# Layer 0's mixer in seven-product units, with two DMA sums each, and the state space half of the output projection among the output gate's products

## The chip, the core and the metric

The kernel runs on one core of one Trainium2 chip. The time is what the device takes for one execution of the whole program, in microseconds (us). TensorE (PE in the profile) multiplies; VectorE (DVE), ScalarE (ACT) and GpSimd (POOL) do the elementwise work; SyncE (SP) issues most of the DMAs. Each engine takes its instructions in the order of its own queue, and semaphores make one engine wait for another.

## The reference

Two layers over 512 tokens of width 1024, all in float32. The change lies in layer 0's mixer: one input projection, split into a state space group (z, xbc, dt) and an mLSTM group (q, k, v, output gate, input and forget gate), whose outputs are concatenated for one output projection.

```python
def hybrid_mixer(h, w_in, conv_w, conv_b, dt_bias, a_log, d_skip, ssd_norm,
                 igate_bias, fgate_bias, mlstm_norm, w_out):
...
    z, xbc, dt_raw, qm, km, vm, om, ig, fg = split_cols(h @ w_in, HY_SPLITS)
    xbc = jax.nn.silu(causal_dwconv(xbc, conv_w, conv_b))
...
    y = y + xs * d_skip.astype(jnp.float32)[:, None]
    gate = jax.nn.silu(z.astype(jnp.float32)).reshape(b, L, SSD_GROUPS, -1)
    y = rms_norm(y.reshape(b, L, SSD_GROUPS, -1) * gate, ssd_norm.reshape(SSD_GROUPS, -1))
    y = y.reshape(b, L, SSD_WIDTH)
    hm = mlstm_chunked(qm.reshape(b, L, ML_HEADS, ML_QK_DIM), km.reshape(b, L, ML_HEADS, ML_QK_DIM),
                       vm.reshape(b, L, ML_HEADS, ML_V_DIM), ig + igate_bias, fg + fgate_bias, ML_CHUNK)
    hm = rms_norm(hm, mlstm_norm.reshape(ML_HEADS, ML_V_DIM)).reshape(b, L, ML_WIDTH)
    hm = hm * jax.nn.sigmoid(om.astype(jnp.float32))
    return jnp.concatenate([y, hm], axis=-1).astype(h.dtype) @ w_out
```

Widths: z 1024, xbc 1536, dt 16, q and k 512 each, v and the output gate 1024 each, two gates of 4; the output projection takes 2048 to 1024. Layer 0 runs a feed-forward block before and after the mixer, and so does layer 1 around its attention.

## The kernel before

**Products in two parts.** Every large product is made of float32 operands split into a high part (a rounding that ScalarE writes) and a low part (what VectorE has left after a subtraction): `split`, L236. `mm3`, L277, is three matmuls: high by high, high by low, low by high. A weight block (128 partitions x 1024 elements, 512 KB) comes by SP's queue into one of four raw buffers (`raw`, L251), and `form`, L257, writes its two parts into one of five form buffers. Both rings are walked in the order in which the program is written, so a buffer's next load or form waits for the last reader of its old content. The third way of `form`, L264 to L266, leaves the subtraction to a DMA: ScalarE writes the negated rounding, a DMA issued by GpSimd adds the raw block to it, and ScalarE writes the rounding. In the mixer of layer 0 it isn't used.

**Seven products.** In the feed-forward blocks most units are done by `seven`, L621: x and a block of weights are each cut in two by two quarters, and seven products of sums of quarters (names A11 to S4, L478) take the place of eight. `xforms`, L572, makes the seven forms of x; differences of weight quarters are made in place by VectorE. The feed-forward blocks and layer 1 have an order written out by a planner (`Plan`, L80) with costs and due times. Layer 0's mixer has none: it is written as generators, and `weave`, L53, gives out steps of one between steps of the other; the framework then orders each engine's queue by a simulated time line, in which what is written earlier goes first where it is ready.

**The mixer**, `hybrid`, L947, in four stretches. First `gates` and `conv` (L1012, six column blocks of 256), on 512-wide products of x times its gain (`xg`); the row of norms (`rrow`) is applied behind the product. Then `ssd` (L1202, 16 steps of 4 blocks by 4 groups of heads) is woven with `projections`: q and k by `gemm_feat`, v and the output gate by `gemm_tok`, L1068, four banks at a time. `decays`, L1235, gets rows of cumulated gates by a broadcast DMA on SP's queue, subtracts on VectorE (L1244), masks on GpSimd, takes the exponential on ScalarE and multiplies on VectorE (L1250, L1253); `outputs`, L1256, has the step's matmuls and their sums (L1268). One step is prepared ahead. Then `mlstm`, L1303, is woven with `gate` (z, L1034). At its end the gated heads are transposed and split (`pht`, L1000). `project`, L898, then runs all 16 row blocks of the output projection, in the order state space first half, mLSTM, state space second half, adds the result to the residual `xT` and prepares x for the next block (`prep`).

PSUM: four banks for large products, four for small ones (`aux`), and pairs of banks (`ps_two`) for the feed-forward units.

## Time and profile before

| | us |
|---|---|
| median of three runs | 2020.58 (2020.55 to 2025.87) |
| profiled execution, its own time | 2019.29 |
| span of that profile, first to last instruction | 2017.6 |
| mean granted clock of TensorE | 0.992 |

The page of a profile gives each engine's busy time and its share of the span, the chain of work that ended last, and groups of instructions: line, engine, operation, what is written from what (partitions x elements), count, then busy time and mean duration in ns, then the engine's idle time just before them and what ended it. Durations of neighbours on one engine overlap, so a price is better read from the distance between two starts in the timeline (start in us from the span's beginning, duration in us, engine, line, operation). L280 to L282 are the three matmuls of every large product. Rows of windows give busy time and counts in a stretch. The mixer of layer 0 lies between about 353 and 757 us.

### The profile page before, as it was taken

Reading aid. Unit: us, or ns where it says so; the run is one execution under the profiler, and the core shown is the slowest. Engines: PE = TensorE matmul, PEld = TensorE weight load, DVE = VectorE, ACT = ScalarE, POOL = GpSimd, SP = SyncE. Lnnn points to the kernel's source line nnn. Section 1 sums busy time; section 2 is a strip of 40 time slices with the busy share of each in tenths; the row PEclk is TensorE's granted clock in tenths of the full one; section 3 lists DMA queues with packets and bytes.
Section 4 is the critical chain, followed back from the end, with each engine's and each line's share of the span. In section 5 each row is a group of like instructions: output and inputs, shape, how many; then the busy total and the mean of one; then the engine's idle time right before and its main releaser. Section 6 shows DMA issues by size and latency. Waiting matters only on the chain.

```text
span 2017.6 us, 34412 instructions
## 1 busy us (share of the span) xinstructions
PE 1984.4 (98%) x13892; PEld 1800.6 (89%) x13892; DVE 1581.4 (78%) x2340; ACT 1170.2 (58%) x1716; POOL 270.1 (13%) x335
## 2 busy tenths in 40 slices
PE   8999999999999999999999999999999999999998
PEld 6999999787788888999998899999965678999998
DVE  6898878886547648988888898978679847988886
ACT  6666657442345434666565575756667644757565
POOL 1000101321101011010002010101215321101010
PEclk9999999999999999999999999999899999999999
DMA  7556566433331232666565356656754202656564
GB/s 210 136 148 167 150 164 148 125 107 115 103 96 63 82 97 63 168 157 162 155 152 149 94 148 167 161 153 160 191 116 105 53 16 69 157 158 165 150 168 115
DMA packets 214439, 265.49 MB, mean 132 GB/s; under 512 B 14140, under 2 KB 187400, under 8 KB 214280
## 3 DMA queue, kind: packets, MB, share of 16 engines
q1 hardware_dynamic: 193632, 190.87, 30.5%
q0 software_dynamic: 20448, 72.36, 19.2%
q8 instruction: 109, 1.79, 0.4%
q14 instruction: 50, 0.41, 0.1%
q10 hardware_dynamic: 200, 0.06, 0.0%
HBM read 188.77 MB, written 2.14 MB: 95 GB/s over the span
## 4 chain that ended last, share of the span: by engine, by line
PE 86%; DVE 5%; DMA 4%; issue 2%; ACT 1%; POOL 1%; SPq 0%; ACTq 0%; POOLq 0%; DVEq 0%
PE pA L281 9%; PE pA L280 9%; PE pA L282 9%; PE pD L280 5%; PE pD L281 5%; PE pD L282 5%; PE pB L280 2%; PE pB L281 2%; PE pB L282 2%; DMA form<-raw 2%; PE po L280 2%; PE po L282 2%; PE po L281 2%; PE ptok L280 2%; PE pu L282 2%
## 5 line engine op out<-in xcount | busy, mean ns | idle before, releaser
L502 DVE TENSOR_TENSOR form<-raw,form 128x1024 fp32r<-128x1024 f32 (+1 forms) x327 | 388.0, 1191 | 113.2 <-ACT form L500 112.3
L500 ACT ACTIVATE form<-raw 128x1024 fp32r<-128x1024 f32 (+1 forms) x327 | 334.6, 1027 | 177.3 <-DVE raw L495 120.6
L280 PE MATMUL pA<-xf,form 128*128 128x256 f32 x1152 | 322.1, 280 | 0.0
L281 PE MATMUL pA<-xf,form 128*128 128x256 f32 x1152 | 321.8, 279 | 0.0
L282 PE MATMUL pA<-xf,form 128*128 128x256 f32 x1152 | 321.4, 279 | 0.0
L495 DVE TENSOR_TENSOR raw<-raw 128x1024 f32<-128x1024 f32 (+2 forms) x241 | 283.6, 1180 | 17.4 <-DMA raw<-in_ffn_w_down 8.6
L530 POOL DMA_DIRECT2D form<-raw x136 | 116.9, 860 | 1202.7 <-ACT form L529 1142.4
L529 ACT ACTIVATE form<-raw 128x1024 fp32r<-128x1024 f32 (+1 forms) x136 | 140.1, 1031 | 140.3 <-PE pD L282 77.4
L280 PEld LDWEIGHTS pA<-xf,form 128*128 128x128 f32 x1152 | 216.4, 188 | 0.2
L282 PEld LDWEIGHTS pA<-xf,form 128*128 128x128 f32 x1152 | 216.1, 188 | 0.0
L281 PEld LDWEIGHTS pA<-xf,form 128*128 128x128 f32 x1152 | 215.8, 187 | 0.2
L281 PE MATMUL pA<-hid,form 128*128 128x256 f32 x704 | 198.6, 282 | 2.8 <-DVE hid L502 2.8
L280 PE MATMUL pA<-hid,form 128*128 128x256 f32 x704 | 198.8, 282 | 0.5 <-ACT hid L500 0.4
L282 PE MATMUL pA<-hid,form 128*128 128x256 f32 x704 | 197.4, 280 | 0.0
L280 PE MATMUL pD<-xf,form 128*128 128x256 f32 x576 | 161.2, 280 | 0.0
L281 PE MATMUL pD<-xf,form 128*128 128x256 f32 x576 | 161.2, 280 | 0.0
L282 PE MATMUL pD<-xf,form 128*128 128x256 f32 x576 | 161.0, 280 | 0.0
L495 DVE TENSOR_TENSOR ft<-ft 128x256 f32<-128x256 f32 (+2 forms) x288 | 146.1, 539 | 4.6 <-ACT ft L748 1.2
L531 ACT ACTIVATE form<-raw 128x1024 fp32r<-128x1024 f32 (+1 forms) x136 | 138.6, 1021 | 0.0
L281 PEld LDWEIGHTS pA<-hid,form 128*128 128x128 f32 x704 | 132.3, 188 | 4.7 <-DVE hid L502 4.6
L280 PEld LDWEIGHTS pA<-hid,form 128*128 128x128 f32 x704 | 132.6, 188 | 1.3 <-ACT hid L500 0.6
L282 PEld LDWEIGHTS pA<-hid,form 128*128 128x128 f32 x704 | 132.3, 188 | 0.0
(447 smaller groups left out, 5191.5 us busy)
## 6 DMA issues: line engine op xcount, KB each, us to landing
form<-raw POOLq DMA_DIRECT2D x120, 512.0 KB, 5.6
raw<-in_ffn_w_gate SPq DMA_DIRECT2D x88, 512.0 KB, 3.8
raw<-in_ffn_w_up SPq DMA_DIRECT2D x88, 512.0 KB, 4.0
raw<-in_ffn_w_down SPq DMA_DIRECT2D x64, 512.0 KB, 4.4
raw<-in_hy_w_in SPq DMA_DIRECT2D x44, 512.0 KB, 3.5
raw<-in_ffn_w_down SPq DMA_DIRECT2D x32, 384.0 KB, 3.4
raw<-in_hy_w_out SPq DMA_DIRECT2D x16, 512.0 KB, 3.3
form<-raw POOLq DMA_DIRECT2D x16, 384.0 KB, 4.2
```

Of the source, the lines that this page charges most:

```text
L280: mm(out, l[0], r[0], start=start, stop=False)
L281: mm(out, l[0], r[1], start=False, stop=False)
L282: mm(out, l[1], r[0], start=False, stop=stop)
L495: (self.p if pool else self.v)(n, lambda: e.tensor_tensor(out(), x(), y(), op=op), reads, writes)
L500: self.s(n, lambda: nc.scalar.activation(hi(), src(), AF.Copy), srck, hik)
L502: n, lambda: nc.vector.tensor_tensor(lo(), src(), hi().bitcast(F32), op=ALU.subtract), srck + hik, lok
L529: self.s(n, lambda: nc.scalar.activation(f()[:, 1], raw, AF.Copy, scale=-1.0), rawk, lok)
L530: self.plan.add("gpsimd", 0.85, lambda: nc.gpsimd.dma_start(f()[:, 1], raw, accum_op=ALU.add), rawk + lok, lok, 5.5)
L531: self.s(n, lambda: nc.scalar.activation(f()[:, 0], raw, AF.Copy), rawk, hik)
```

## The change

The products of v, k, z and the output gate become seven-product units of 512 columns (`seven_now`): two for v, one for k, two for z, two for the output gate. The seven forms of x, now with the norm applied, are made by `xforms_now` in four row groups, woven among convolution and q. In each unit the forms of two blocks go by the DMA sum; among convolution and q the second half of each weight block does (`early`). The scratch tiles of scan and mLSTM move into one large tile (`room`). The scan's and mLSTM's subtractions become biases of four narrower exponentials, and three of the scan's steps are prepared ahead instead of one. mLSTM's output is written over v, and its norm and the output gate are multiplied in behind the gate's products. `project` becomes a generator and is called twice: the state space half from two raw and two form buffers of its own (`side`), woven with the output gate's units, and the mLSTM half at the end. A second sum into the residual comes with the second call.

```diff
-NMIX = dict(mix0=10, mix1=15)
+NMIX = dict(mix0=12, mix1=15)
...
-        r = self.rings[which]
+        r = self.rings[self.side + which]
...
-        if self.stage == "mix1":
+        if self.stage == "mix0" and self.summing:
             nc.scalar.activation(f[:, 1], raw, AF.Copy, scale=-1.0)
             nc.gpsimd.dma_start(f[:, 1], raw, accum_op=ALU.add)
             nc.scalar.activation(f[:, 0], raw, AF.Copy)
...
-    def wload(self, src):
+    def wload(self, src, side=""):
 
         n = src.shape[0] // P
         for k in range(0, n, 4):
-            yield self.form(self.raw(src[k * P : (k + 4) * P].rearrange("(k p) n -> p k n", p=P), 4, 256))
+            self.summing, self.side = self.early and k == 4, side
+            f = self.form(self.raw(src[k * P : (k + 4) * P].rearrange("(k p) n -> p k n", p=P), 4, 256))
+            self.side = ""
+            yield f
...
+    ROOMS = dict(rows=(0, 512, 1024), ce=(1536, 2048, 2560), xd=(3072, 4096), st=(5120,), btok=(6144,), cbs=(6400,), v=(6656,),
+                 mrows=(0, 512), qs=(1536, 2048), ktok=(3072, 3584), hst=(5120,), kept=(1024, 2560, 4096, 4608))
+
+    def room(self, kind, *shape):
+        if self.rooms is None:
+            self.rooms = self.big.tile([P, 10768], F32, name="rooms", tag="rooms", bufs=1)
+
+            with self.tc.issue_after(self.ready.ins):
+                self.nc.vector.memset(self.rooms[:, 0:10752:256], 0.0)
+        self.count[kind] = i = self.count.get(kind, -1) + 1
+        at = self.ROOMS[kind][i % len(self.ROOMS[kind])]
+        dims = {f"a{j}": x for j, x in enumerate(shape)}
+        names = " ".join(dims)
+        return self.rooms[:, at : at + math.prod(shape)].rearrange(f"p ({names}) -> p {names}", **dims)
...
-    def project(self, w, hid, scale, nxt, cuts, group=1):
+    def project(self, w, hid, nxt, cuts, group=1, side=""):
...
-            po = {(dp, m): self.mmps("po") for dp in dps for m in range(2)}
+            po = {(dp, m): self.aux("po", (T,)) if side else self.mmps("po") for dp in dps for m in range(2)}
...
+                    yield
...
-        weave(
-            self.gates(w, ((0, DT0, 16), (16, F0, 4), (20, I0, 4)), g),
-            chain(*(self.conv(w, X0, cp, xs, bc) for cp in (4, 5, 0, 1, 2, 3))),
-            1.0,
-        )
...
+        gates, xf = self.gates(w, ((0, DT0, 16), (16, F0, 4), (20, I0, 4)), g), []
+
+        def early():
+            for cp in (4, 5, 0, 1, 2, 3):
+                yield from self.conv(w, X0, cp, xs, bc)
+            for cp in range(2):
+                W = list(self.wload(w[:, Q0 + cp * 256 : Q0 + cp * 256 + 256]))
+                for m in range(2):
+                    ps = self.mmps("pqk")
+                    self.gemm_feat(ps, W, m)
+                    self.mark = nc.vector.scalar_tensor_tensor(
+                        q[:, 2 * cp + m], ps, 128 ** -0.5, self.rrow, op0=ALU.mult, op1=ALU.mult
+                    )
+                    yield
+
+        early, self.early = early(), True
+        weave(gates, early, 1.0)
+        weave(early, self.xforms_now(xf), 0.4)
+        self.early = self.summing = False
...
+        act, tt = nc.scalar.activation, nc.vector.tensor_tensor
+
+        def kept(dest):
+
+            def keep(i, ps):
+                act(dest(*((1, 0), (0, 1), (1, 1))[i]), ps, AF.Copy)
+
+            def done(a, j, ps):
+                if (a, j) == (1, 0):
+                    act(dest(1, 0), ps, AF.Copy)
+                else:
+                    tt(dest(a, j), ps, dest(*((1, 0) if a + j == 0 else (a, j))), op=ALU.add)
+
+            return keep, done
...
             for h in (0, 2):
+                yield from self.seven_now(w, V0 + h * 256, xf, True, *kept(lambda a, j, h=h: v[a][:, :, h + j, 0:256]))
+            yield from self.seven_now(w, K0, xf, False, *kept(lambda a, j: k[:, 2 * j : 2 * j + 2, a * H : a * H + H]))
...
+        weave(self.ssd(xs, bc, g), values(), 1.8)
...
+        def passing(use, f):
+
+            tiles = {}
+
+            def keep(i, ps):
+                t = tiles[((0, 0), (0, 1), (1, 1))[i]] = self.room("kept", 2, H)
+                act(t, ps, AF.Copy)
+
+            def done(a, j, ps):
+                if (a, j) == (1, 0):
+                    t = self.room("kept", 2, H)
+                    act(t, ps, f)
+                else:
+                    t = tiles.pop((a, j))
+                    tt(t, ps, t, op=ALU.add)
+                    act(t, t, f)
+                use(a, j, t)
+
+            return keep, done
+
+        def output_gate():
             for h in (0, 2):
...
-        weave(self.ssd(xs, bc, g), projections(), 1.35)
...
+                def gated(a, j, o, h=h):
+                    for b in range(2):
+                        x = v[a][:, b, h + j, 0:256]
+                        nc.vector.scalar_tensor_tensor(
+                            x, x, rs[2 * a + b][:, h + j : h + j + 1], o[:, b], op0=ALU.mult, op1=ALU.mult
+                        )
+
+                yield from self.seven_now(w, O0 + h * 256, xf, True, *passing(gated, AF.Sigmoid))
+
+        mlstm = self.mlstm(q, k, v, rs, g)
+        zgate = self.gate(w, Z0, xs, hid, xf, passing)
+        weave(mlstm, zgate, 1.5)
+        wo = a["hy_w_out"][0]
+        x = self.slot("side")
+        self.rings["sideraw"] = [0, [x[:, 2 * i : 2 * i + 2].rearrange("p a b -> p (a b)") for i in range(2)]]
+        self.rings["sideany"] = [0, [
+            self.slot("side", F32R).rearrange("p (i a) b -> p i (a b)", i=2) for i in range(2)
+        ]]
+        weave(self.project(wo, hid, None, ((0, 4), (4, 8)), 1, "side"), output_gate(), 2.0)
+        hh, hl = self.feat("hh", KC, F32R), self.feat("hl", KC, F32R)
+        for c in range(KC):
+            pt = self.aux("pht", (T,))
+            for b in range(NB):
+                nc.tensor.transpose(
+                    pt[:, b * P : (b + 1) * P], v[b // 2][:, b % 2, c // 2, (c % 2) * P : (c % 2 + 1) * P], self.ident
+                )
+            self.split_gain(hh[c], hl[c], pt, self.par[:, 116 + c : 117 + c])
+            hid[KC + c] = (hh[c], hl[c])
+        drain(self.project(wo, hid, nxt, ((8, 12), (12, 16)), 2))
...
+    def xforms_now(self, xf):
+
+        nc = self.nc
+        tt = nc.vector.tensor_tensor
+        tiles = [self.part.tile([P, 2, 4, H], F32R, name="xf", tag="xf", bufs=7) for _ in range(7)]
+        row = self.rrow.rearrange("p (a b) -> p a b", a=2)
+        for q in range(4):
+            t = self.big.tile([P, 8, H], F32, name="fx", tag="fx", bufs=1)
+            for m in range(2):
+                nc.vector.scalar_tensor_tensor(
+                    t[:, 2 * m : 2 * m + 2], self.xT[:, 2 * q + m].rearrange("p (a b) -> p a b", a=2),
+                    self.gain(self.which, 2 * q + m), row, op0=ALU.mult, op1=ALU.mult,
+                )
+            yield
+            tt(t[:, 4], t[:, 1], t[:, 3], op=ALU.add)
+            tt(t[:, 5], t[:, 4], t[:, 0], op=ALU.subtract)
+            tt(t[:, 6], t[:, 0], t[:, 1], op=ALU.subtract)
+            tt(t[:, 7], t[:, 2], t[:, 5], op=ALU.subtract)
+            for form, i in ((self.A11, 0), (self.A12, 2), (self.A22, 3), (self.S1, 4), (self.S2, 5), (self.S3, 6), (self.S4, 7)):
+                self.ready = self.split(tiles[form][:, 0, q], tiles[form][:, 1, q], t[:, i])
+                if i in (3, 5, 7):
+                    yield
+            xf.append(lambda i, q=q: (tiles[i][:, 0, q], tiles[i][:, 1, q]))
+
+    def seven_now(self, w, c0, xf, rows, keep, done):
...
+        nc = self.nc
+        less = lambda o, x, y: nc.vector.tensor_tensor(o, x, y, op=ALU.subtract)
+        b11, b21, b12, b22 = (
+            self.raw(w[:, c0 + j * 256 : c0 + j * 256 + 256].rearrange("(q two p) n -> two p q n", two=2, p=P)[par], 4, 256)
+            for j in range(2) for par in range(2)
+        )
+
+        def made(block, summed=False):
+            self.summing = summed
+            return self.form(block)
+
+        def mul(ps, f, form, start):
+            for s in range(2):
+                part = slice(s * P, (s + 1) * P)
+                for q in range(4):
+                    x, b = xf[q](form), (f[0][:, q], f[1][:, q])
+                    l, r = (x, b) if rows else (b, x)
+                    self.mm3(
+                        ps[:, s, 0:H], tuple(y[:, part] for y in l), r, start and q == 0, q == 3, more=not start
                     )
-                self.split_gain(hh[c], hl[c], pt, self.par[:, 116 + c : 117 + c])
-                hid[KC + c] = (hh[c], hl[c])
-                if c % 2:
-                    yield
-
-        weave(mlstm(), self.gate(w, Z0, xs, hid), 0.8)
-        self.project(a["hy_w_out"][0], hid, 1.0, nxt, ((0, 4), (8, 16), (4, 8)), 2)
+            return ps[:, :, 0:H]
+
+        pair = lambda: self.ps_two.tile([P, 2, T], F32, name="pw", tag="pA")
+        A = pair()
+        keep(0, mul(A, made(b11), self.A11, True))
+        yield
+        B = pair()
+        done(0, 0, mul(B, made(b21), self.A12, True))
+        yield
+        less(b11, b12, b11)
+        less(b12, b22, b12)
+        f22 = made(b22)
+        less(b22, b22, b11)
+        keep(1, mul(A, made(b22), self.S2, False))
+        yield
+        D = pair()
+        less(b21, b21, b22)
+        keep(2, mul(D, made(b11), self.S1, True))
+        yield
+        f12, f21 = made(b12, True), made(b21, True)
+        done(1, 1, mul(A, f12, self.S3, False))
+        yield
+        done(0, 1, mul(D, f22, self.S4, False))
+        yield
+        done(1, 0, mul(A, f21, self.A22, False))
+        yield
+        self.summing = False
...
+            def gated(a, j, o, grp=grp, ssq=ssq):
+                x, part = xs.tiles[grp][:, 2 * j : 2 * j + 2, a * H : a * H + H], ssq[:, a * H : a * H + H]
+                tt(x, x, o, op=ALU.mult)
+                act(o, x, AF.Square)
+
+                if a == j:
+                    tt(part, o[:, 0], o[:, 1], op=ALU.add)
+                else:
+                    tt(o[:, 0], o[:, 0], o[:, 1], op=ALU.add)
+                    tt(part, part, o[:, 0], op=ALU.add)
+
+            yield from self.seven_now(w, Z0 + grp * 512, xf, False, *passing(gated, AF.Silu))
...
+        ts(dense, dense, -1.0, None, op0=ALU.mult)
+        g["nacs"] = dense
...
-            tt(e, rows, g["acs"][:, c, hs].unsqueeze(2).to_broadcast([P, 4, P]), op=ALU.subtract)
...
+            for j in range(4):
+                nc.scalar.activation(e[:, j], rows[:, j], AF.Exp, bias=g["nacs"][:, c, 4 * q + j : 4 * q + j + 1])
...
-        ahead = decays(0, 0)
+        ahead = [decays(0, 0)]
...
+            while len(ahead) < 3 and i + len(ahead) < len(steps):
+                c1, q1 = steps[i + len(ahead)]
+                if not q1:
+                    block(c1)
+                ahead.append(decays(c1, q1))
...
-                tt(oc[:, h], oc[:, h], pn[:, 0:256], op=ALU.mult)
...
+                nc.scalar.activation(vc[:, h, 0:256], pn[:, 0:256], AF.Copy)
...
-            tt(oc, oc, r.unsqueeze(2).to_broadcast([P, 4, 256]), op=ALU.mult)
+            rs.append(r)
```

More of the change, by code (lines that the diff above doesn't have):

```diff
@@ L780, in prep_later @@
             self.xgn = [[Lazy(lambda: self.part.tile([P, 4, T], F32R, name="xgn", tag="xg")) for _ in range(2)] for _ in range(2)]
+            if which == 4:
+                xgn4 = Lazy(lambda: self.big.tile([P, 2, KC, T], F32R, name="xgn", tag="xg4", bufs=1))
+                self.xgn = [[lambda i=i, j=j: xgn4()[:, i, 4 * j : 4 * j + 4] for j in range(2)] for i in range(2)]
             squares4 = Lazy(lambda: self.tmp.tile([P, 4, T], F32, name="ssq", tag="ssq", bufs=1))
@@ L908, in project @@
                     col = slice(dp * 256, (dp + 1) * 256)
[L909 removed]
+                    for i, f in enumerate(self.wload(w[c0 * P : c1 * P, col], side)):
                         for m in range(2):
@@ L1205, in ssd @@
         tt = nc.vector.tensor_tensor
[L1207 to L1216 removed]
+        btok, cbs = (self.room(n, 2, P) for n in ("btok", "cbs"))
+        xd = [self.room("xd", 16, 64) for _ in range(NB)]
         st = None
@@ L1272, in state @@
         def state(c):
+            pt = self.aux("pbt", (2, P))
+            for n in range(2):
+                nc.tensor.transpose(pt[:, n], bc[:, n, c * P : (c + 1) * P], self.ident)
+            nc.scalar.activation(btok, pt, AF.Copy)
             xe = xd[c]
             tt(xe, xe, g["de"][:, c].unsqueeze(2).to_broadcast([P, 16, 64]), op=ALU.mult)
-            new = st if c else self.tmp.tile([P, 16, 64], F32, name="st", tag="st", bufs=1)
+            new = st if c else self.room("st", 16, 64)
             if c:
@@ L1280, in state @@
                 psl = self.aux("psl", (8, 64))
-                nc.tensor.matmul(psl, btok[:, c, n], xe[:, 8 * n : 8 * n + 8], start=True, stop=True)
+                nc.tensor.matmul(psl, btok[:, n], xe[:, 8 * n : 8 * n + 8], start=True, stop=True)
                 o = new[:, 8 * n : 8 * n + 8]
```

193 lines of the change are left out of this document (45 added, 148 removed).

## The prediction

> **What bounds the kernel now.** The page comes first: the busy times, then the chain of work that ended last.
>
> ```profile
> PE 1984.4 (98%) x13892; PEld 1800.6 (89%) x13892; DVE 1581.4 (78%) x2340; ACT 1170.2 (58%) x1716; POOL 270.1 (13%) x335
> PE 86%; DVE 5%; DMA 4%; issue 2%; ACT 1%; POOL 1%; SPq 0%; ACTq 0%; POOLq 0%; DVEq 0%
> ```
>
> TensorE sets the end. The windows show it stage by stage; columns are the stretch, its length, then PE, PEld, DVE, ACT and POOL busy time with counts, the granted clock, DMA share, GB/s. The first two are feed-forward (seven-product) stretches, the other four layer 0's mixer: convolution and q (called E below), k, values and output gate beside the state space scan (S), z gate beside mLSTM (M), output projection.
>
> ```profile
> 100.88:151.32 50.44, 49.34 (x415) 48.94 (x414) 47.20 (x59) 30.42 (x40) 3.94 (x5) 1.00 0.58 148
> 201.76:252.20 50.44, 50.44 (x429) 50.40 (x428) 44.38 (x55) 33.53 (x43) 5.15 (x6) 1.00 0.59 150
> 378.20:458.00 79.80, 79.80 (x382) 65.21 (x382) 69.33 (x125) 36.17 (x47) 21.52 (x16) 1.00 0.34 103
> 458.00:597.00 139.00, 139.00 (x746) 107.83 (x743) 76.53 (x119) 52.80 (x71) 14.57 (x15) 1.00 0.34 108
> 597.00:664.50 67.50, 67.50 (x329) 56.88 (x328) 49.75 (x104) 32.03 (x80) 6.72 (x6) 1.00 0.17 55
> 664.50:757.00 92.50, 92.50 (x420) 75.99 (x419) 44.84 (x60) 34.11 (x45) 8.63 (x6) 1.00 0.31 98
> ```
>
> In the mixer TensorE is never idle, so time leaves only through less TensorE work, and every wait that the new form adds is lost in full. VectorE is at 87% in E and 55 to 74% after it: there is room, but not much of it early.
>
> **Products removed.** A product's duration in the groups overlaps the next one, so its price is the distance between starts. Rows of the timeline:
>
> ```profile
> 458.95 0.39 PE L280 MATMUL pqk<-xgn,form 128*128 128x512 f32 x1
> 463.08 0.40 PE L280 MATMUL pqk<-xgn,form 128*128 128x512 f32 x1
> 559.63 0.40 PE L281 MATMUL ptok<-form,xgn 128*128 128x512 f32 x1
> 570.36 0.40 PE L282 MATMUL ptok<-form,xgn 128*128 128x512 f32 x1
> ```
>
> Between the first pair lie 18 starts: 4.13/18 = 0.229 us. Between the second, 46: 10.73/46 = 0.233 us. A 256-column matmul costs 50.44/429 = 0.1176 us by the second window above, where weight loads fill all the time (PEld 50.40): half the columns cost 0.50 to 0.51 of the time. A unit of 512 columns has 96 wide matmuls now (8 row blocks x 4 column blocks x 3) and 7 x 24 = 168 narrow ones after, 19.76 us. The four units of values and output gate save 96 x 0.233 - 19.76 = 2.6 us each; k and z's two 96 x 0.229 - 19.76 = 2.2 us each. Sum **10.4 + 6.6 = 17 us**. The projection keeps its 384 wide products, whatever their order; its transposes and the scan's matmuls stay. Without any new wait: 2019.3 - 17 = 2002.3 us.
>
> **Work added on VectorE and ScalarE**, which has to stay hidden. VectorE's operations:
>
> ```profile
> 217.65 0.69 DVE L495 TENSOR_TENSOR ft<-pB,ft 128x512 f32<-128x512 f32 x1
> 218.26 1.22 DVE L495 TENSOR_TENSOR raw<-raw 128x1024 f32<-128x1024 f32 x1
> 219.39 0.42 DVE L502 TENSOR_TENSOR hid<-ft,hid 128x256 fp32r<-128x256 f32 x1
> 229.64 0.42 DVE L495 TENSOR_TENSOR ft<-ft 128x256 f32<-128x256 f32 x1
> 229.97 0.68 DVE L502 TENSOR_TENSOR hid<-ft,hid 128x512 fp32r<-128x512 f32 x1
> ```
>
> Start to start: 512 wide 0.61, 1024 wide 1.13, 256 wide 0.33 us. A unit has five low parts by VectorE, five differences and three sums out of PSUM: 10 x 1.13 + 3 x 0.61 = 13.1 us, against 4 x 1.13 = 4.5 us and evacuations now. Two low parts a unit are made by ScalarE and an adding DMA.
>
> E: the new transforms of x are 8 scaled copies (512 wide), 16 sums and 28 low parts (256 wide): 8 x 0.61 + 44 x 0.33 = 19.4 us. They start once the row of norms is there, as the first use of that row does now:
>
> ```profile
> 379.36 0.68 DVE L1022 TENSOR_TENSOR u<-pxbc,raw 128x512 f32<-128x512 f32 x1
> ```
>
> From there on VectorE has 79.8 - 69.3 = 10.5 us idle in E; the second half of each weight block goes to the adding DMA, some 6 blocks after 378, which frees 6.8 us. It is 2 us short, and the first value product needs all four row groups and its own 1.13 us low part. I take **4 us** of wait; bounds 0 (the scan's transposes fill it) and 8.
>
> S: of its 139.0 us, 384 value and output gate products take 89.5 and 96 of k 22.0, so the scan's matmuls take 27.5. After: 3 x 19.76 + 27.5 = 87 us. The scan's VectorE rows:
>
> ```profile
> L1244 DVE TENSOR_TENSOR arow<-arow,raw 128x512 f32<-128x512 f32 x16 | 12.2, 765 | 3.4 <-DMA arow<-arows 2.5 <-ACT ce L1242 0.9
> L1250 DVE TENSOR_TENSOR arow<-arow,btok 128x512 f32<-128x512 f32 x16 | 10.7, 688 | 6.2 <-ACT arow L1249 6.0 <-ACT btok L1233 0.3
> L1268 DVE SCALAR_TENSOR_TENSOR xs<-xs,raw,py 128x128 f32<-128x128 f32 x32 | 9.5, 343 | 22.4 <-PE py L1265 22.4
> L1253 DVE TENSOR_TENSOR ce<-ce,bc 128x512 f32<-128x512 f32 x12 | 8.2, 684 | 0.0
> ```
>
> L1244 goes into the exponential's bias. The other three are 28 us, the states and scaled inputs (26 operations of 512 width, 0.61 us) 16 us; with overlap 39 us. With three units 39 + 39 = 78 us, 90% of 87. The nearest stretch of that load is the first feed-forward window: VectorE 47.20 of 50.44 us (94%), TensorE 1.1 us idle, 2.2%. I take that share, **2 us**; bounds 0 and 15%, 13 us, if decays and sums queue behind each other.
>
> M: of 67.5 us, 192 z products take 44, so mLSTM has 23.5; after, 39.5 + 23.5 = 63 us. VectorE: two units 26, the z chain and its sums of squares 9, the rest of now's 49.75 (less eight low parts 9, z's two passes 10, squares 4, output gate multiplies 10) 17, the normalisation's part 5: 57 us, 90%. ScalarE, and its table loads:
>
> ```profile
> L239 ACT ACTIVATE form<-raw 128x1024 fp32r<-128x1024 f32 x60 | 63.2, 1057 | 114.0 <-PE ptok L282 34.3 <-PE po L281 29.7 <-PE pxbc L281 15.4
> L385 ACT ACTIVATE yh<-xs,raw 128x512 fp32r<-128x512 f32 x8 | 5.2, 716 | 1.4 <-DVE xs L1064 1.4
> 655.73 1.95 ACT L385 ACTIVATE yh<-xs,raw 128x512 fp32r<-128x512 f32 x3
> 624.72 1.28 ACT L1336 ACT_TABLE_LOAD   x1
> 626.01 0.63 ACT L1336 ACTIVATE qs<-qs 128x512 f32<-128x512 f32 x1
> L1249 ACT ACTIVATE arow<-arow 128x512 f32<-128x512 f32 x16 | 10.0, 628 | 22.6 <-POOL arow L1245 22.6
> L1356 ACT ACTIVATE hsq<-pn 128x256 f32<-128x256 f32 x16 | 6.0, 377 | 0.0
> ```
>
> Three of 0.72 us end after 1.95, so each overlaps the next by 0.1. A unit has nine 1024-wide passes (0.96) and eleven 512-wide (three copies, four silus, four squares, about 0.52): 14 us; the high parts of y, mLSTM's exponentials, copies, squares and their sums add 22: 50 us. Exponentials of mLSTM and silus of z alternate: four to eight loads of 1.28 us, 5 to 10 us, so 55 to 60 of 63. The exponentials become four 128-wide ones; from 628 and 377 ns for 512 and 256 I estimate 0.25 us each, 1.0 for 0.63, some 7 us over S, where ScalarE has room. Wait taken for M: **2 us**, bounds 0 and 9 (15%). By the rows a load is followed 1.29 us later by its exponential. [...]
>
> Projection's first half among the output gate's products: 39.5 + 192 x 0.229 = 83.5 us TensorE; VectorE has two units 26, eight low parts 9, eight more sums into x 5, sixteen gate products 5: 45 us. It hides; without that cover the extra sums cost 5 us. The last gate product is followed by sigmoid, multiply, transpose, two splits, some 3 us; the 48 wide products of the heads done before (11 us) cover it. Taken 0, bounds -1 and 3.
>
> Queues: an adding DMA and the loads.
>
> ```profile
> form<-raw POOLq DMA_DIRECT2D x120, 512.0 KB, 5.6
> raw<-in_hy_w_in SPq DMA_DIRECT2D x44, 512.0 KB, 3.5
> ```
>
> The four weight loads of the next unit stand on SP's queue in ring order; the second waits until the second adding DMA has landed, and behind it stand the other two and the scan's row broadcasts, which the decays wait for. On POOL's queue each adding DMA waits for ScalarE's negated copy, and the scan's selects, which the exponentials wait for, stand behind it. A product is 24 x 0.1176 = 2.8 us; the first adding DMA has four products (11.3 us) for a 0.96 pass, 5.6 us of landing and issue. It fits.
>
> Sum: 2019.3 - 17 + 4 + 2 + 2 = **2010.3 us**. The profiled execution (2019.29) is 1.3 below the median of the three runs (2020.58), less than matters; I forecast 2010.
>
> **Rivals.** *All hidden*: E fills with scan matmuls, 2002 us. For it: feed-forward hides the same units at 88%. Against: there nothing else shares VectorE.
>
> *The mixed stages are bound by VectorE and ScalarE*: S and M lose half of their upper bounds, 6.5 + 4.5, and E its 8 us: 2019.3 - 17 + 19 = 2021, no change.
>
> *The form ring stalls each unit (slower)*. Five form buffers, seven forms a unit: b22's form is held until the sixth product, and the next unit's first form takes its buffer. Only the seventh product (2.8 us) covers a ScalarE pass (0.96) and a low part (1.13): 0.7 us spare. From one 1.13 us VectorE operation ahead in the queue on, TensorE waits. Two or three ahead make 2 us, and a wait also costs the clock:
>
> ```profile
> 1433.00:1445.00 12.00, 8.62 (x49) 8.51 (x48) 12.00 (x15) 7.00 (x15) 6.08 (x6) 0.72 0.67 195
> ```
>
> Here 3.4 us idle is followed by a mean clock of 0.72 over 12 us, 3.4 us more. With 2 us of each, seven units cost 7 x 4 = 28, with E's 4: 2019.3 - 17 + 32 = 2034 us. For it: VectorE at 90%. Against: the scan's and mLSTM's own matmuls can stand between two units. [...]
>
> *It does not do what it says*, that narrow products cost more than 0.1176 here: nothing in the rows for it.
>
> **Chances.** Forecast 0.47 (0.42 of it faster, 0.05 within), all hidden 0.12, no change 0.13, ring 0.28. A change of 0.3% (6 us) is what a measurement can tell: faster 0.54, same 0.18, slower 0.28. The forecast's own range is 2004 to 2017; with the other cases 1998 to 2037.
>
> **What will show it.** Narrow starts 0.118 us apart in the new units; the mixer ending 9 us earlier, by the first gate product of the next feed-forward stage, now
>
> ```profile
> 756.56 0.40 PE L280 MATMUL pg<-xgn,form 128*128 128x512 f32 x1
> ```
> further one TensorE gap near 460 before the first value product. Gaps at unit boundaries after the sixth product, ended by VectorE's low part, with the clock under 1.00, would mean the ring. VectorE above 95% in S or M would mean the no-change case. I am wrong if the new waits exceed 17 us.

## The result and the profile after

| | before | after |
|---|---|---|
| median of four runs on one chip, us | 2020.57 (2018.37 to 2025.87) | 2043.55 (2041.02 to 2046.84) |
| profiled execution, us | 2019.29 | 2041.02 |
| span of that profile, us | 2017.6 | 2039.2 |

Slower: a ratio of 1.0111, 95% interval 1.0086 to 1.0135. The forecast was 2010 us, faster.

The page of the changed kernel, busy times and chain of waits:

```profile
PE 1976.3 (97%) x14394; PEld 1822.5 (89%) x14394; DVE 1623.3 (80%) x2417; ACT 1243.6 (61%) x1888; POOL 296.1 (15%) x357
PE 79%; DMA 7%; DVE 6%; issue 4%; ACT 3%; POOL 1%; SPq 0%; ACTq 0%; POOLq 0%; DVEq 0%
```

TensorE's share of the chain fell from 86 to 79%, and DMA rose most, from 4 to 7%. The windows, as before (stretch, length, PE, PEld, DVE, ACT and POOL busy with counts, granted clock, DMA share, GB/s): E; then S, from the first value unit to the first z unit; M, to the first output gate unit; the units of the output gate with the projection's first half; its last half; the feed-forward stage behind the mixer.

```profile
380.00:456.00 76.00, 76.00 (x330) 61.06 (x329) 73.39 (x142) 38.51 (x62) 26.94 (x17) 1.00 0.41 110
456.00:559.80 103.80, 90.39 (x736) 83.01 (x735) 71.62 (x122) 59.31 (x118) 17.83 (x20) 0.95 0.51 130
559.80:640.80 81.00, 73.40 (x542) 67.56 (x542) 58.43 (x105) 64.13 (x149) 15.39 (x13) 0.98 0.35 95
640.80:735.70 94.90, 88.76 (x544) 80.36 (x543) 55.35 (x82) 41.82 (x55) 6.74 (x7) 0.96 0.48 134
735.70:782.70 47.00, 47.00 (x225) 39.26 (x224) 26.09 (x36) 19.78 (x28) 7.61 (x5) 1.00 0.30 90
782.70:1455.40 672.70, 670.29 (x5299) 651.89 (x5297) 579.51 (x733) 423.55 (x564) 69.93 (x74) 1.00 0.57 147
```

Before, TensorE was busy through all four stretches of the mixer. Now it is idle for 27.2 us (13.4 in S, 7.6 in M, 6.1 beside the output gate), and the clock is below 1 in those same three. No other engine is full there: VectorE 69 and 72%, ScalarE 57 and 79% in S and M. The mixer, from its gate product to the first feed-forward product, took 403.3 us (353.0 to 756.3) and takes 427.8 (354.9 to 782.7), 24.5 more. The products did become cheaper:

```profile
458.98 0.28 PE L284 MATMUL pw<-form,xf 128*128 128x256 f32 x1
462.34 0.28 PE L285 MATMUL pw<-form,xf 128*128 128x256 f32 x1
```

Between these two starts lie 28 steps, 3.36/28 = 0.120 us each, where I had taken 0.1176 from the feed-forward stages. 1176 such matmuls at 0.0024 more make 2.8 us, so the products saved 14 us instead of 17, and the new waits in the mixer cost 24.5 + 14 = 38.5 us, where I had forecast 8.

What TensorE, then ScalarE, waits for between 456 and 735 us (engine, tile, line, releaser; us in total, times, longest):

```profile
PE pw L283 <- ACT rooms L1010: 5.5, 3, 4.1
PE pw L283 <- ACT form L239: 5.5, 5, 2.0
PE py L1352 <- DVE rooms L1339: 4.2, 1, 4.2
PE pw L283 <- ACT rooms L981: 3.7, 1, 3.7
PE pw L283 <- ACT k L981: 3.1, 2, 2.6
```

```profile
ACT rooms L1331 <- DMA rooms<-arows: 22.4, 10, 5.1
...
ACT form L239 <- DMA raw<-in_hy_w_in: 10.3, 3, 7.6
ACT form L239 <- PE pw L285: 8.1, 2, 6.8
ACT rooms L1338 <- POOL rooms L1333: 7.7, 5, 4.1
```

Of TensorE's 27 us of waits, 20 end with ScalarE: with copies of products out of PSUM (L981, L1010) and with high parts (L239). The 4.2 us end with VectorE's multiplication of the scan's last decays (L1339). ScalarE's longest waits among the scan and the units are at the scan's exponentials (L1331, L1338), whose rows are not there; the lines left out are waits of the projection's own forms (`side`). The chain of waits shows one such stall, in order of time (start, us, what):

```profile
492.45 5.66 DMA rooms<-arows
...
498.85 1.15 POOL rooms L1333
...
500.02 1.29 ACT rooms L1338 x4
...
501.63 4.98 DMA rooms<-arows
...
506.69 0.07 ACT rooms L1331
...
507.23 0.59 ACT rooms L981
...
507.86 0.58 PE pw L283
```

The product that L981 copies ended at 498.5, but the copy stands behind L1331 in ScalarE's queue, which waits 5.1 us for its rows; the next product into that bank waits 3.7 us, and starts at half clock (0.58 us for a matmul of 0.28). The broadcast of these rows was issued late, at 501.6. Ahead of it in SyncE's queue stood weight loads that waited for the landing of adding DMAs; SyncE's waits between 492.5 and 502:

```profile
SPq L254 <- DMA form<-raw: 6.5, 2, 5.0
```

The longest wait beside the output gate has a like form: from 657.5 to 661.6 TensorE waits for a copy (L1010) that stands behind a high part (L239), which itself waited 7.6 us for its weight block. And the 4.2 us in M are the scan's last exponentials, which stand behind two table loads (ACT_TABLE_LOAD, 1.28 us each, ahead of a silu and behind it) and mLSTM's exponentials. The transfers themselves have become slower too. DMA queues and issues between 458 and 597 before, and 456 and 560 after (packets, MB, share of the 16 engines' time; KB each, median us to landing):

```profile
q1 hardware_dynamic: 9932, 14.94, 34.0%
raw<-in_hy_w_in SPq DMA_DIRECT2D x20, 512.0 KB, 3.5
arow<-arows SPq DMA_DIRECT2D x9, 256.0 KB, 3.9
```

```profile
q1 hardware_dynamic: 8608, 10.27, 32.8%
q0 software_dynamic: 864, 3.15, 17.2%
raw<-in_hy_w_in SPq DMA_DIRECT2D x12, 512.0 KB, 4.8
rooms<-arows SPq DMA_DIRECT2D x15, 256.0 KB, 5.7
form<-raw POOLq DMA_DIRECT2D x6, 512.0 KB, 5.5
```

q0 carries the adding DMAs: 3.15 MB in 17.2% of 104 us, 5.7 us of all engines for a MB, against 3.3 on q1. A broadcast takes 5.7 instead of 3.9 us to land, a weight load 4.8 instead of 3.5.

### The profile page after: what moved, and what is told of

It is laid out like the page before. It is cut to its first block, busy times and chain, and to the rows that moved or that the text cites. A ratio compares the mean times of both kernels' runs of the same rounds, so it can differ in the third digit from the quotient of the medians.

```text
span 2039.2 us, 35744 instructions
## 1 busy us (share of the span) xinstructions
PE 1976.3 (97%) x14394; PEld 1822.5 (89%) x14394; DVE 1623.3 (80%) x2417; ACT 1243.6 (61%) x1888; POOL 296.1 (15%) x357
## 3 DMA queue, kind: packets, MB, share of 16 engines
q8 instruction: 113, 1.85, 0.4%
## 4 chain that ended last, share of the span: by engine, by line
PE 79%; DMA 7%; DVE 6%; issue 4%; ACT 3%; POOL 1%; SPq 0%; ACTq 0%; POOLq 0%; DVEq 0%
PE pA L284 9%; PE pA L283 9%; PE pA L285 9%; PE pD L283 4%; PE pD L285 4%; PE pD L284 4%; PE pB L283 2%; PE pB L285 2%; PE pB L284 2%; DMA form<-raw 2%; PE po L283 2%; PE po L284 2%; PE po L285 2%; PE pu L283 1%; PE pu L285 1%
## 5 line engine op out<-in xcount | busy, mean ns | idle before, releaser
L283 PEld LDWEIGHTS pA<-xf,form 128*128 128x128 f32 x1152 | 219.3, 190 | 0.2
L284 PEld LDWEIGHTS pA<-xf,form 128*128 128x128 f32 x1152 | 219.3, 190 | 0.2
L285 PEld LDWEIGHTS pA<-xf,form 128*128 128x128 f32 x1152 | 219.3, 190 | 0.0
L284 PEld LDWEIGHTS pA<-hid,form 128*128 128x128 f32 x704 | 133.0, 189 | 4.8 <-DVE hid L521 4.7
L665 ACT ACTIVATE ft<-pA 128x512 f32<-128x512 f32 x120 | 71.5, 596 | 104.7 <-PE pA L285 97.3
L283 PEld LDWEIGHTS pA<-hid,form 128*128 128x128 f32 x704 | 133.0, 189 | 2.1 <-ACT hid L519 1.0
```

The lines of the kernel that those rows point to most:

```text
L283: mm(out, l[0], r[0], start=start, stop=False)
L284: mm(out, l[0], r[1], start=False, stop=False)
L285: mm(out, l[1], r[0], start=False, stop=stop)
L665: self.s(T, lambda: nc.scalar.activation(to(), ps()[:, :, 0:H], AF.Copy), [(*psk, 0), (*psk, 1)], tok)
```

## The experiments

Ratios are against the kernel before on the same chip, with 95% intervals; 0.001 is 2 us. The changed kernel stands at 1.0111. Stage lengths are from each run's trace, with borders as above; M contains the scan's last steps. The framework lays out the queues anew for every kernel, so no edit leaves all other order as it was. Four theories of the lost time: A, ScalarE's queue stands behind late broadcasts; B, the ring of forms; C, VectorE; D, the adding DMAs, either by holding SyncE's queue, since a load waits there for their landing (D1), or by their traffic (D2).

**e1_rows**

```diff
+        fetched = [fetch(*s) for s in steps[:2]]
...
-            rows = self.rows_from(g["arows"][c, hs], "rows")
```

> A fourth room for the scan's row broadcasts, and each broadcast issued one step ahead of its exponentials. Theory A (ScalarE's in-order queue: the units' keep copies and high parts stand behind exponentials that wait for late broadcasts, 22 us of such waits in the changed kernel): the waits of the exponentials for broadcasts fall below 8 us, and 8 to 20 us go, 2024 to 2036. Rival B (ring of forms) and rival C (VectorE is the bound of the mixed stages): 2041 to 2046, whatever the waits for broadcasts do.

2054.78 us, 1.0176 (1.0156 to 1.0195). ScalarE's waits between 456 and 735 us:

```profile
ACT form L239 <- DMA raw<-in_hy_w_in: 19.4, 5, 4.3
ACT rooms L1334 <- DMA rooms<-arows: 6.1, 2, 3.2
```

The exponentials' wait fell from 22.4 to 6.1 us as meant, and the wait of the high parts for weight loads rose from 10.3 to 19.4. S took 102.9 us, as much as before the edit. The time lies outside both predicted cases, part of it through the wider tile (see e17). Late issue of the broadcasts is not by itself the cause; early ones push the loads back. Theory A falls in that form.

**e2_onerow** (every step reads one loaded row room, `one`; fifteen broadcasts are left out, and with them the later steps' own rows)

> One broadcast instead of sixteen: every step of the scan reads the rows of the first (its values are then those of the first step; every instruction of ScalarE, VectorE and TensorE remains). Theory A: no exponential waits for a broadcast any more, and the whole of what the waits cost goes, 12 to 25 us: 2019 to 2032. Rival B and rival C: 2041 to 2046, since the work of every engine is the same. If late broadcasts are only one of several releasers, 5 to 12 us go.

2035.20 us, 1.0079 (1.0060 to 1.0098), in the third case; S 91.8 us. Against its control (e17) the gain is 15 us, as theory A had it, but by taking 15 transfers away, not by having them early: weight loads landed in 3.6 us, the adding DMAs in 5.0.

**e3_nosum**

```diff
-        f12, f21 = made(b12, True), made(b21, True)
+        f12, f21 = made(b12), made(b21)
```

> The two low parts that adding DMAs form in each unit are formed by VectorE again (14 adding DMAs and 14 negating copies of ScalarE less; VectorE gets 14 subtractions of 1.1 to 1.2 us more). If the adding DMAs' traffic and the loads held behind them cause the waits (theory D): 2025 to 2038. Rival C (VectorE the bound): 16 us more work on the bound, 2052 to 2062. Theory A without D: ScalarE is relieved by 14 x 1 us and its exponentials still wait, 2036 to 2044.

2025.43 us, 1.0037 (1.0021 to 1.0052): 15 us gone. S and M of this kernel, and its transfers in S:

```profile
455.50:546.90 91.40, 86.86 (x736) 80.36 (x735) 78.86 (x128) 54.18 (x111) 16.21 (x14) 0.98 0.37 114
546.90:625.80 78.90, 71.66 (x542) 66.19 (x541) 62.27 (x109) 62.97 (x151) 11.74 (x9) 1.00 0.23 71
```

```profile
raw<-in_hy_w_in SPq DMA_DIRECT2D x12, 512.0 KB, 4.3
rooms<-arows SPq DMA_DIRECT2D x15, 256.0 KB, 4.5
```

S is 12.4 us shorter although VectorE has 7 us more to do in it (78.9 for 71.6). Theory C falls for S; theory D stands, with both parts open.

**e4_side** (the output gate's units drained alone, then the projection in one piece)

> The giving out undone: the output gate's units run alone, and the whole output projection follows them in the main rings. The stage of the output gate took 95 us in the trace where 83.5 were worked out. If the side part costs (side rings of two, aux PSUM, ScalarE's high parts of both streams): the two parts together are 8 to 12 us shorter, 2031 to 2036. If giving out covers the units' own waits: longer by 5 to 10 us, 2048 to 2054.

2047.58 us, 1.0141 (1.0114 to 1.0168), an interval that overlaps the changed kernel's. The stretch from the first output gate unit to the mixer's end took 145.1 us instead of 141.9. The time lies under the second case, and giving out the projection is not where the time went.

**e5_swap**

```diff
+        at = [0, 3, 2, 1] if self.swapped else [0, 1, 2, 3]
```

> Adding DMAs and all other work as in the changed kernel; only the raw buffers of a unit's second and fourth block change places from unit to unit, so that a unit's second load (needed by its second product) goes into the buffer that is released in the middle of the unit before, and no longer waits for the landing of the last adding DMA. Theory D1 (the landings hold SyncE's queue, and with it the loads and broadcasts behind): 6 to 14 us go, 2028 to 2036 where the changed kernel stands at 2042. Theory D2 (the adding DMAs' traffic slows the other transfers): 2039 to 2045.

2044.14 us, 1.0126 (1.0100 to 1.0152): no gain. But the edit didn't take the hold away; it moved it to another load. SyncE's waits for landings between 456 and 735 us, in the changed kernel and in e5:

```profile
SPq L254 <- DMA form<-raw: 54.0, 14, 8.1
```

```profile
SPq L254 <- DMA form<-raw: 52.9, 14, 8.1
```

So which load is held makes no difference; D1 itself isn't tested by this run. e2 bears on it: there SyncE waits for landings 59.3 us, and S is short all the same, so held weight loads alone do not cost.

**e6_rowq** (a fourth room; broadcasts issued by ScalarE)

> The row broadcasts are issued by ScalarE's queue, into four rooms, so that they stand behind no load. Theory D1: they are no longer late, 5 to 12 us go, 2030 to 2037. Theory D2: they take as long as before to land, and ScalarE's issues are added, 2040 to 2050.

2051.42 us, 1.0157 (1.0128 to 1.0186), as its control e17. S was 103.2 us and the exponentials waited only 1.9 us for broadcasts in it, so the broadcasts' place behind held loads isn't the whole cost either, with the reserve that ScalarE now issues them and that its high parts waited 8.6 us for loads. D1 and D2 are not separated by these runs.

**e7_neg** (the negated copy stays on ScalarE, the sum goes back to VectorE)

> The two low parts of each unit by VectorE as in the run without adding DMAs (2025), but ScalarE still writes the negated copy that is then overwritten: ScalarE has the changed kernel's work, the adding DMAs are gone. Theory D (the adding DMAs): 2024 to 2029. Theory A' (ScalarE's two more copies a unit, 14 x 1 us in its in-order queue): 2035 to 2044.

2032.42 us, 1.0061 (1.0041 to 1.0080), between the two cases. S and M:

```profile
455.40:545.40 90.00, 86.44 (x736) 78.89 (x734) 75.59 (x125) 58.45 (x115) 16.20 (x14) 1.00 0.37 113
545.40:628.70 83.30, 74.84 (x538) 70.14 (x534) 61.85 (x106) 65.47 (x145) 9.45 (x9) 0.92 0.23 70
```

Without adding DMAs S is short with ScalarE's copies too, so in S the adding DMAs are the cost. Of e3's 15 us some 10 belong to them. The other 5, ScalarE's copies, lie within the overlap of the two intervals. M (83.3 us) and the rest of the mixer (142.1) are no shorter than in the changed kernel (81.0 and 141.9): no gain from the missing adding DMAs shows there.

**e8_nosum_swap**

> No adding DMAs in the units, and the exchanged raw buffers too. If loads held by late buffers still cost without the adding DMAs: 2013 to 2022. If the loads are then early enough: 2023 to 2027, as without the exchange.

2029.64 us, 1.0048 (1.0032 to 1.0064), over both cases and as e3 within the intervals: the exchange brings nothing here either.

What is left after e3 lies in M. Its exponentials and silus alternate; rows of ScalarE's timeline in e3:

```profile
563.47 1.27 ACT L1338 ACTIVATE rooms<-rooms,raw 128x128 f32<-128x128 f32 x4
564.75 1.28 ACT L1019 ACT_TABLE_LOAD   x1
566.05 0.63 ACT L1019 ACTIVATE rooms<-rooms 128x512 f32<-128x512 f32 x1
566.70 1.28 ACT L1423 ACT_TABLE_LOAD   x1
567.99 1.28 ACT L1423 ACTIVATE rooms<-rooms,raw 128x128 f32<-128x128 f32 x4
```

Two table loads, 2.56 us, stand around one silu of 0.63. There are nine such loads in this stage.

**e9_tanh**, on e3; **e12_tanh_sum**, on the changed kernel

```diff
-                tt(x, x, o, op=ALU.mult)
+                nc.vector.scalar_tensor_tensor(x, x, 0.5, z, op0=ALU.mult, op1=ALU.mult)
...
+                nc.vector.scalar_tensor_tensor(x, o, 1.0, x, op0=ALU.add, op1=ALU.mult)
...
-            yield from self.seven_now(w, Z0 + grp * 512, xf, False, *passing(gated, AF.Silu))
+            yield from self.seven_now(w, Z0 + grp * 512, xf, False, *passing(gated, AF.Tanh, first, 0.5))
```

> Without adding DMAs in the units, and z's silu written as 0.5 z (1 + tanh(z/2)), so that ScalarE need not load tables between mLSTM's exponentials and z's silus: ten loads of 1.28 us less in the z gate's stage, eight VectorE passes of 0.68 us more. Theory S (that stage, 79 us without adding DMAs where 63 were worked out, is bound by ScalarE and its table loads): 6 to 12 us go, 2014 to 2020 where the run without adding DMAs stood at 2025. Rival V (VectorE binds that stage): 2025 to 2032.

> The changed kernel with tanh for silu and nothing else. Theory S: 6 to 12 us go from the z gate's stage, 2031 to 2037 where the changed kernel stands at 2042. Rival V: 2042 to 2048.

e9: 2020.84 us, 1.0005 (0.9992 to 1.0019), at the upper end of theory S's case; e12: 2041.12, 1.0131 (1.0082 to 1.0180), just under rival V's. M of e9, then of e12:

```profile
547.70:620.80 73.10, 70.86 (x543) 66.13 (x542) 63.22 (x110) 49.17 (x136) 13.22 (x9) 1.00 0.25 76
```

```profile
566.70:647.60 80.90, 73.20 (x534) 68.66 (x534) 59.09 (x107) 52.73 (x134) 13.41 (x13) 0.94 0.36 95
```

ScalarE loses 11 to 14 us in both; the stage is 6 us shorter in e9 and not at all in e12 (3 us of which may be the lower clock of e12's profiled execution, the longest of its runs). With the adding DMAs there, ScalarE's load alone is not what sets M's length, as far as one trace and e12's wide interval show. M's transfers, in the changed kernel and in e9:

```profile
raw<-in_hy_w_in SPq DMA_DIRECT2D x8, 512.0 KB, 7.3
```

```profile
raw<-in_hy_w_in SPq DMA_DIRECT2D x8, 512.0 KB, 4.2
```

The same eight weight loads land in 7.3 us beside four adding DMAs and in 4.2 without (5.4 in e3, 4.1 in e7, whose M was no shorter for it).

**e10_sumMO** (`made(b12, self.sums_on)`, false until M begins), and **e11_tanh_sumMO** with tanh too

> Adding DMAs only in the z and output gate units; v, v and k have both low parts by VectorE. If the adding DMAs cost where they meet the scan's row broadcasts (the scan's stage was 104 us with, 91 and 90 us without them): 2026 to 2032, the scan's stage 90 to 93 us. If they cost in each unit alike (14 us over seven units): 2033 to 2038.

> The two edits together: tanh for silu, adding DMAs only in the z and output gate units, where VectorE is thereby relieved of 8 low parts. If VectorE is the next bound in the z gate's stage: 2 to 6 us under the run with tanh and no adding DMAs. If ScalarE's two extra copies a unit weigh more: 2 to 6 us over it.

e10: 2032.38 us, 1.0067 (1.0046 to 1.0088), S 91.2 us. e11: 2032.87, 1.0073 (1.0054 to 1.0093), M 80.5 us. e10 lies between its two cases; e11 lies outside both, some 14 us over e9. Taking the adding DMAs out of v, v and k brings some 9 us. Taking them and ScalarE's copies out of z and the output gate brings another 6, and only then does tanh bring 6. Since e7, with the copies and without adding DMAs in any unit, stands where e10 does (1.0061 and 1.0067), these 6 us may be the copies' as well; copies with tanh and no adding DMAs weren't run.

**e13_tanh_rows**, **e14_tanh_pool** and **e15_all**, on e9 (e14: `nc.gpsimd.tensor_tensor` for the sums of squares)

> No adding DMAs in the units, tanh for silu (2021 us), and the fourth room with broadcasts one step ahead. With the adding DMAs, broadcasts ahead of time only moved the waits to the weight loads. If what is left in the scan's stage (93 us, 87 worked out) is still late broadcasts: 2015 to 2019. If not: 2020 to 2025.

> As the run with tanh, and the sums of squares of z's groups are added by GpSimd instead of VectorE (12 additions of 0.33 us). VectorE is busy without a break from 623 to 634 and TensorE waits 5 us there, at the border of the z gate and the output gate. If VectorE binds that border: 2015 to 2019. If GpSimd's additions come later than VectorE's did: 2021 to 2026.

> Both of these edits together: if both gains hold and add, 2010 to 2016; if neither, 2021 to 2027.

2030.45 us, 1.0066 (1.0048 to 1.0085); 2022.19, 1.0019 (1.0006 to 1.0032); 2027.71, 1.0057 (1.0037 to 1.0077). None gains, and e13 lies outside both its cases. e13's mixer took 411.1 us and e9's 409.5; most of its loss lies elsewhere, and by e17 the wider tile could be 8 us of it.

**e16_tanh_noearly**, on e9

```diff
-            self.summing, self.side = self.early and k == 4, side
+            self.summing, self.side = False, side
```

> As the run with tanh, and the adding DMAs of the convolution and q weights are taken out too, so that layer 0's mixer has none. VectorE gets 8 low parts of 1.13 us in a stage where it has about 10 us idle and the transforms to hide: if the forecast's account of that stage holds, 4 to 10 us slower, 2025 to 2031; if VectorE has more room there than I worked out, 2018 to 2023.

2031.98 us, 1.0074 (1.0055 to 1.0092), 14 us over e9 and more than forecast. So in E, where VectorE was busy 73.4 of 76 us in the changed kernel, the adding DMAs earn their price as far as the whole time goes. Where the 14 us lie is less clear: the first unit starts 17 us earlier in this layout, E and S together are only 4 us longer than in e9, and M, which the edit doesn't touch, is 8 us longer at a lower clock (0.94).

**e17_room**, the control (10768 to 11280 columns, the added ones unused)

> The changed kernel with a tile of rooms 512 columns wider, of which nothing uses the added part: a control for the runs with a fourth room or one broadcast, whose feed-forward stage after the mixer was 3.4 us longer in the trace than that of the runs without it. If the wider tile alone does that: 2045 to 2048, and 3.4 us of their times are not the broadcasts'. If the edits did it: 2041 to 2045.

2051.72 us, 1.0152 (1.0127 to 1.0177), over both cases: some 8 us for a wider tile alone, though the interval just overlaps the changed kernel's; in the trace the mixer is 3.1 us longer, and the rest lies outside. So e1 and e6 are to be read against 1.0152, not 1.0111 (each the same within the intervals), and e2's 1.0079 is 15 us under it, as much as e3 gained.

**e18_ratio**, on e9 (1.8 to 1.4)

> As the run with tanh and no adding DMAs in the units (2021 us), and 1.4 instead of 1.8 products given out at each of the scan's steps, so that they reach to its end. If what is left in the scan's stage (6 us over the forecast) comes from products crowding its first steps: 2013 to 2018. If it comes from each product's own passes in the queues: 2019 to 2024.

2026.60 us, 1.0035 (1.0017 to 1.0053), over both cases; S 97.8 us instead of 92.7: worse.

No kernel beats the one before. e9 equals it, 21 us under the change as made (0.0106 of 2020), but its mixer is still 6 us longer than before (409.5 against 403.3); the rest of the kernel is shorter by 4.

## Why the prediction was wrong

Forecast and measured mixer stages in us; the forecast lengths are those of before with the prediction's terms.

| | forecast | after | e3 | e9 |
|---|---|---|---|---|
| E (105 + 4) | 109 | 101.1 | 102.6 | 102.6 |
| S (87 + 2) | 89 | 103.8 | 91.4 | 92.7 |
| M (63 + 2) | 65 | 81.0 | 78.9 | 73.1 |
| output gate and projection (83.5 + 92.5 - 192 x 0.229) | 132 | 141.9 | 138.1 | 141.1 |
| sum | 395 | 427.8 | 411.0 | 409.5 |

**Products**: right in kind; 14 us instead of 17, since a narrow matmul costs 0.120 here.

**E, 4 us of wait**: wrong the other way. The last product of q starts at 456.04 and the first unit right behind it; the transforms were ready. The stage is 8 us under the forecast, because 24 of the scan's output matmuls, and some transposes with them, that lay in it before now lie in S. Some of S's excess is that move, so S is best read with E: 7 us over. In the same way 64 of the scan's output matmuls and four others, some 7 us, lie in M now and none did before, so that much of M's excess is the scan's.

**"It fits"** is the step that failed. I held each adding DMA against its own deadline, 11.3 us, which it met (none of TensorE's waits ends with one), and priced what it does to others at nothing. In S that price is 12 to 14 us (e3, e7, e10). S took 102.9 to 109.2 us in the seven traces with them and with all broadcasts, and 90.0 to 93.5 in nine without them there; e16 and e18 give work out in another way. Taking the 14 adding DMAs of the units away together with ScalarE's copies gives back 15 us of the whole (e3), with the copies left in 10 (e7); taking 15 broadcasts away instead also gives 15 (e2 against e17). By which way they cost is open. The transfers beside them land later: in S 5.7 us for a row, where e3 has 4.5 and the kernel before 3.9, and 4.8 for a weight block, where e3 has 4.3 and the kernel before 3.5; so part of the delay is there without adding DMAs. And SyncE's queue waits for their landings, which I had named as an order and also priced at nothing: e2 shows no cost of it for loads, e6, with its reserve, not the whole cost for broadcasts, and the stall shown above has it (6.5 us). Neither was varied by itself. For M and the output gate a cost of the adding DMAs apart from their copies isn't shown (e7).

**S, 2 us of wait, from VectorE's 90%**: wrong releaser. VectorE was busy 69%, and S became shorter when it got more to do. Of TensorE's 13.4 us of waits in S 12 end with ScalarE. In 5.7 of them the copy or high part stands behind exponentials whose rows came late, in 2.6 behind a high part whose weight block came late; in the other 5 it is ScalarE's and VectorE's own work. I had reckoned ScalarE's busy time and not what stands behind a waiting instruction in its queue.

**M, 2 us**: 16 us over, some 7 of them the scan's matmuls. ScalarE's load was reckoned nearly right (55 to 60 of 63; it is 64.1 of 81), and its table loads cost 6 us on the path (e9), but only once the adding DMAs and their copies are gone (e11, e12).

**Output gate and projection, 0**: 10 us over. Undoing the giving out doesn't help (e4), nor does GpSimd for VectorE's sums at the border (e14). e9 still has 9 of the 10; what holds them stays open, as do 5 us in E to M, of which 2 are the price of the narrow products.

**Outside the mixer**, which I took as unchanged, the span is 2.9 us shorter: 2039.2 - 427.8 = 1611.4 against 2017.6 - 403.3 = 1614.3. The feed-forward stage behind the mixer takes 672.7 instead of 677.4; e17 shows that the width of one tile alone moves such amounts.

**The rivals.** The ring of forms came nearest with its time, 2034, but that is mostly luck: TensorE's waits that ended with VectorE's low part, the sign I had named for it, come to 1.1 us in S. ScalarE's forms did wait for TensorE's release (8.1 us in the line above, 6 more at L264 and L266), and the number of form buffers wasn't varied. Its second half, that waits cost clock, came true: 20.5 us at half clock in the mixer, in which TensorE was busy 17.8 us, so some 9 us. The rival of VectorE and ScalarE was half right, for M. I had put the limit of 17 us beyond which I would be wrong; the new waits were 38.5.

## What to carry to other kernels

A DMA that takes work from an engine can be paid by the other transfers of that stretch: price it by the loads and broadcasts that share the DMA engines with it or stand behind its landing in a queue, not only by its own deadline. Here it cost 12 to 14 us where broadcasts ran (S), a row landing in 5.7 us where it took 4.5 without (e3), and taking it out of E, where VectorE was nearly full, cost 14 us of the whole. In front of an in-order queue, list for each instruction that can wait what stands behind it; a copy that frees PSUM, behind an exponential that waits for a DMA, stopped TensorE for 3.7 us at once in a stage in which ScalarE was busy 57% of the time. In the mixed stage M, where exponentials and silus alternate, ScalarE had a table load of 1.28 us at each turn (nine in e3); taking the silus' loads out gave 6 us once the adding DMAs and their copies were gone (e9) and nothing that showed with them there (e12).

## What the runs showed of the hardware

The half-clock stretches of the changed kernel's mixer begin at 482.9, 506.8, 581.9 and 660.4 us: 7, 22 and 23 times 3.41 us apart. They last 3.41 us or twice that:

```profile
482.88:486.29 3.41, 3.38 (x16) 3.38 (x17) 3.38 (x5) 0.40 (x1) 0.00 (x0) 0.50 0.00 0
506.77:513.60 6.83, 5.74 (x36) 5.52 (x38) 5.07 (x7) 4.58 (x9) 1.15 (x1) 0.50 0.00 0
581.87:585.28 3.41, 3.07 (x22) 2.77 (x23) 1.53 (x5) 3.41 (x8) 0.00 (x0) 0.50 0.08 26
660.37:667.20 6.83, 5.63 (x26) 5.47 (x26) 6.14 (x9) 5.91 (x9) 0.00 (x0) 0.50 0.26 80
```

The 3.41 us ahead of each, then two such stretches that were not followed by half clock:

```profile
479.47:482.88 3.41, 1.24 (x6) 0.84 (x6) 3.41 (x5) 1.81 (x5) 0.00 (x0) 1.00 0.00 0
503.36:506.77 3.41, 0.83 (x5) 0.41 (x4) 0.00 (x0) 0.08 (x1) 0.00 (x0) 1.00 0.76 205
578.46:581.87 3.41, 0.00 (x0) 0.00 (x0) 1.20 (x2) 3.40 (x11) 1.15 (x1) 1.00 1.02 339
656.96:660.37 3.41, 0.52 (x5) 0.31 (x3) 0.00 (x0) 0.40 (x1) 0.00 (x0) 1.00 0.77 158
```

```profile
493.11:496.52 3.41, 1.97 (x16) 1.97 (x17) 3.41 (x7) 3.41 (x5) 1.30 (x2) 1.00 1.09 256
547.73:551.14 3.41, 1.85 (x16) 1.65 (x14) 1.37 (x2) 1.79 (x5) 0.00 (x0) 1.00 0.63 197
```

With the mixer divided into stretches of 3.413 us from 482.88 both ways, those at full clock with TensorE busy for 1.24 us or less were followed by half clock, those with 1.85 or more were not. (Two stretches already at half clock, with 2.32 and 2.21 us, were followed by another.) In three of the four TensorE was not idle throughout. Ahead of 482.9 its waits were 1.38, 0.36 and 0.72 us, and 3.41 us at half clock followed.
